# A scheduling priority for the input projection's matmuls in a four-mixer decoder layer

## The chip, the cores and the metric

One core of a Trainium2 chip runs the whole kernel. The metric is device time in microseconds (us); before the change the median of three runs is 2140.05 us (2138.56 to 2140.4). The core has five engines that run side by side, each through its own queue in order: TensorE (PE, matmuls, with its weight loads shown apart as PEld), VectorE (DVE), ScalarE (ACT), GpSimd (POOL) and SyncE (SP, which issues most of the transfers). An engine whose next instruction waits for another engine holds everything behind it in its queue.

## The reference

For 2048 rows of 1024 numbers the reference computes one decoder layer:

```
u     = rmsnorm(x) ;  proj = u @ w_in              # 1024 x 7712
y     = concat( GLA(..), mLSTM(..), HGRN2(..), Mamba-2 SSD(..) )   # 512 columns each
h     = x + y @ w_out ;  out = rmsnorm(h)
```

Each of the four mixers is a causal recurrence over time, computed in chunks: inside a chunk of 128 rows a masked product of queries and keys (scores) times the values, between chunks a state that is decayed and added to. GLA and HGRN2 have a decay for each channel, which the kernel handles by a ladder of levels (1, 2, 4, ... 64 rows apart), each with a small matmul and elementwise rescaling of keys and queries before the next.

## The kernel before

The 2048 rows are worked through in two halves of 1024 rows (8 chunks). In each half ten units run in this order: g0, g1 (GLA, two heads each), s0, s1 (SSD, four heads each), h0 to h3 (HGRN2, one head each), m0, m1 (mLSTM, two heads each). After both halves, the output phase multiplies y by w_out.

A unit has two parts, and in the text of the program the second follows the first.

- **Projections.** Groups of 256 columns of `proj`. Each number is split into a high and a low part, so each product takes three matmuls over 8 slices of the contraction: 24 matmuls for one accumulation. `proj_chan` (line 256) and `proj_chan2` (line 267) put 128 channels by 512 rows in one PSUM bank (tile `ps_c`), four banks and 96 matmuls for a group; `proj_tok` (line 279) puts 128 rows by 256 channels in half a bank (tile `ps_t`, in g0 `ps_g`), 192 matmuls for a group. The PSUM tiles carry the tag `proj`, which has four banks. ACT and DVE move each finished bank into SBUF: an h unit projects `hqf` into `qp`, `kb` and `f`, then `hvz` into `v` and `sz`; an s unit `sx`, `sbc` (through a four-tap convolution, `conv_silu2`) and `sz`; a g unit `gqk`, `gv`, `gz`; an m unit, for each of its two heads, `mqk` and `mvo`, and `mz` at the end. The weights of a group are loaded one group ahead, into two buffers.
- **Products.** What the mixer does with them: `lin_unit` (line 441) for g and h, with tiles `ps_s`, `ps_kt`, `ps_u`, `ps_o`; the loop over 8 chunks in `ssd` (`ps_xt`, `ps_s`, `ps_o`, `ps_u`); the rest of `mlstm`. They use the other four PSUM banks, tag `t`. They are small matmuls, between which DVE and ACT work: each level of `lin_unit` must wait until DVE has rescaled `kb` and `qf`, and that waits until the level before has read them.

SBUF tiles with few buffers tie the units together: `qp`, `kb`, `f` and `v` have two buffers each, `sz` four, `qf` and `pl` one. A g unit takes both `v` buffers; an s unit keeps a `qp`, `kb`, `v` and `f` buffer until its last chunk; an h unit gives `f` back after level 1, `qp` after level 2, `kb` near its end and `v` at its end.

**The order of the work** is not written by hand. Tile's planner makes each engine's queue at build time: it plays the program through with estimated durations, and gives an engine that is free the ready instruction with the lowest priority number. That number is a counter which goes up by one with each instruction of the program's text. So before the change the products of a unit come in front of the next unit's projections whenever they are ready, and a projection runs when no product is.

Of the kernel before, what the change touches and what calls it, by code (L numbers as in the profile page):

```python
# [21 lines left out]
P = 128  # L22
S = 2048
D = 1024
KT = D // P
# [91 lines left out]
class Kernel:  # L117
    def __init__(self, tc, a):
        self.tc, self.nc, self.a = tc, tc.nc, a

    def mm(self, out, l, r, start=True, stop=True, shared=False):

        self.nc.tensor.matmul(out, l, r, start=start, stop=stop, skip_group_check=shared)  # L123
# [132 lines left out]
    def proj_chan(self, w, c, b):  # L256

        hi, lo = w
        ps = self.psp.tile([P, 512], F32, tag="proj", name="ps_c")
        cs = slice(c * P, (c + 1) * P)  # L260
        for k in range(KT):
            self.mm(ps, hi[:, k, cs], self.uh[b][:, k], start=k == 0, stop=False)
            self.mm(ps, hi[:, k, cs], self.ul[b][:, k], start=False, stop=False)
            self.mm(ps, lo[:, k, cs], self.uh[b][:, k], start=False, stop=k == KT - 1)
        return ps

    def proj_chan2(self, w, b):

        hi, lo = w
        pss = [self.psp.tile([P, 512], F32, tag="proj", name="ps_c") for _ in range(2)]  # L270
        for k in range(KT):
            for c, ps in enumerate(pss):
                cs = slice(c * P, (c + 1) * P)
                self.mm(ps, hi[:, k, cs], self.uh[b][:, k], start=k == 0, stop=False)
                self.mm(ps, hi[:, k, cs], self.ul[b][:, k], start=False, stop=False)
                self.mm(ps, lo[:, k, cs], self.uh[b][:, k], start=False, stop=k == KT - 1)
        return pss

    def proj_tok(self, w, ps, t):

        hi, lo = w
        b, ts = t // 4, slice(t % 4 * P, t % 4 * P + P)
        for k in range(KT):
            self.mm(ps, self.uh[b][:, k, ts], hi[:, k], start=k == 0, stop=False)
            self.mm(ps, self.uh[b][:, k, ts], lo[:, k], start=False, stop=False)
            self.mm(ps, self.ul[b][:, k, ts], hi[:, k], start=False, stop=k == KT - 1)

    def proj_tok2(self, w):

# [876 lines left out]
```

## Time and profile before

| | before |
|---|---|
| median of 3 runs | 2140.05 us |
| profiled execution, its own time | 2138.02 us |
| its span, first to last instruction | 2136.2 us |
| granted TensorE clock, mean over the span | 0.994 |
| PE busy | 2095.6 us (98%), 14014 matmuls |
| DVE busy | 1206.0 us (56%) |
| ACT busy | 750.8 us (35%) |

Busy time is the time in which an engine has an instruction of the program in work. Matmuls overlap in the records, so that the sum of their durations is above the busy time; the pace of a run of matmuls is read from a stretch that holds only them. A row of a window gives its start and end, its length, the busy time of PE, PEld, DVE, ACT and POOL with the number of instructions (an engine without any may be missing), the granted clock as a share of full speed, the share of the DMA engines' time, and GB/s; asked for one tile, only the instructions that write or read it are counted.

### The profile page before, as it was taken

Reading aid. Unit: us, or ns where it says so; the run is one execution under the profiler, and the core shown is the slowest. Engines: PE = TensorE matmul, PEld = TensorE weight load, DVE = VectorE, ACT = ScalarE, POOL = GpSimd, SP = SyncE. Lnnn points to the kernel's source line nnn. Section 1 sums busy time; section 2 is a strip of 40 time slices with the busy share of each in tenths; the row PEclk is TensorE's granted clock in tenths of the full one; section 3 lists DMA queues with packets and bytes.
Section 4 is the critical chain, followed back from the end, with each engine's and each line's share of the span. In section 5 each row is a group of like instructions: output and inputs, shape, how many; then the busy total and the mean of one; then the engine's idle time right before and its main releaser. Section 6 shows DMA issues by size and latency. Waiting matters only on the chain.

```text
span 2136.2 us, 35274 instructions
## 1 busy us (share of the span) xinstructions
PE 2095.6 (98%) x14014; PEld 1869.4 (88%) x14014; DVE 1206.0 (56%) x2860; ACT 750.8 (35%) x1885; POOL 62.1 (3%) x96
## 2 busy tenths in 40 slices
PE   8999999999999999999999999999999999999998
PEld 7888889898899999997979889999899998888887
DVE  4564868657676555525366966565654555433332
ACT  6531433444444335442222333333433344212111
POOL 0000011100000000000000211000000000000000
PEclk9999999999999999999999999999999999999999
DMA  8533344444244354442314334322323336423321
GB/s 288 197 94 126 89 152 145 148 140 130 71 130 149 129 159 167 131 143 62 89 51 136 87 105 110 91 82 60 109 90 98 101 109 199 140 80 96 102 74 50
DMA packets 223094, 251.47 MB, mean 118 GB/s; under 512 B 145224, under 2 KB 156600, under 8 KB 211664
## 3 DMA queue, kind: packets, MB, share of 16 engines
q1 hardware_dynamic: 216448, 229.80, 35.3%
q10 hardware_dynamic: 6480, 19.40, 2.6%
q8 instruction: 110, 1.80, 0.3%
q14 instruction: 56, 0.46, 0.1%
HBM read 160.70 MB, written 88.45 MB: 117 GB/s over the span
## 4 chain that ended last, share of the span: by engine, by line
PE 88%; DVE 5%; ACT 3%; DMA 3%; issue 1%; SPq 0%; POOL 0%; ACTq 0%; DVEq 0%; POOLq 0%
PE ps_t L123 30%; PE ps_c L123 25%; PE ps_out L123 15%; PE ps_o L123 6%; PE ps_s L123 5%; PE ps_u L123 3%; PE ps_g L123 2%; DMA ST<-w_out 1%; DMA t2k<-xT 1%; DVE kb L512 1%; DMA hi<-wk 1%; DVE ST L494 0%; ACT t2k L620 0%; DVE ST L557 0%; PE ps_xt L894 0%
## 5 line engine op out<-in xcount | busy, mean ns | idle before, releaser
L123 PE MATMUL ps_t<-hi,uh 128*128 128x256 f32 x1920 | 545.5, 284 | 0.0
L123 PE MATMUL ps_t<-hi,ul 128*128 128x256 f32 x1920 | 544.8, 284 | 0.0
L123 PE MATMUL ps_t<-lo,uh 128*128 128x256 f32 x1920 | 544.3, 284 | 0.0
L123 PEld LDWEIGHTS ps_t<-hi,uh 128*128 128x128 f32 x1920 | 368.0, 192 | 1.6 <-issue 0.7
L123 PEld LDWEIGHTS ps_t<-lo,uh 128*128 128x128 f32 x1920 | 368.1, 192 | 0.9
L123 PEld LDWEIGHTS ps_t<-hi,ul 128*128 128x128 f32 x1920 | 368.0, 192 | 0.3
L123 PE MATMUL ps_c<-uh,hi 128*128 128x512 f32 x896 | 358.7, 400 | 7.4 <-ACT uh L155 7.4
L123 PE MATMUL ps_c<-ul,hi 128*128 128x512 f32 x896 | 357.7, 399 | 0.0
L123 PE MATMUL ps_c<-uh,lo 128*128 128x512 f32 x896 | 356.9, 398 | 0.0
L123 PEld LDWEIGHTS ps_c<-uh,hi 128*128 128x128 f32 x896 | 170.4, 190 | 41.1 <-ACT uh L155 7.8
L123 PEld LDWEIGHTS ps_c<-ul,hi 128*128 128x128 f32 x896 | 170.6, 190 | 34.8 <-DVE ul L156 1.2
L123 PEld LDWEIGHTS ps_c<-uh,lo 128*128 128x128 f32 x896 | 170.5, 190 | 33.9
L305 ACT ACTIVATE v<-ps_t,ss 128x128 f32<-128x128 f32 x128 | 40.4, 363 | 157.8 <-PE ps_t L123 157.7
L976 DVE TENSOR_TENSOR o_sz<-o_sz,ps_out 128x512 f32<-128x512 f32 (+1 forms) x33 | 22.1, 671 | 129.8 <-PE ps_out L123 127.5
L123 PE MATMUL ps_out<-woh,o_qp 128*128 128x512 f32 x288 | 94.3, 396 | 0.5 <-ACT woh L936 0.5
L300 ACT ACTIVATE sz<-ps_t,ss 128x128 f32<-128x128 f32 (+1 forms) x160 | 54.5, 388 | 89.6 <-PE ps_t L123 82.2
L254 DVE TENSOR_TENSOR lo<-raw,hi 128x1024 fp32r<-128x1024 f32 (+1 forms) x58 | 70.5, 1225 | 17.9 <-ACT hi L252 17.0
L301 DVE SCALAR_TENSOR_TENSOR sz<-sz,ps_t 128x256 f32<-128x256 f32 (+1 forms) x80 | 37.5, 471 | 70.6 <-ACT sz L300 70.2
L123 PE MATMUL ps_out<-woh,o_v 128*128 128x512 f32 (+1 forms) x213 | 75.4, 389 | 0.0
L252 ACT CAST hi<-raw 128x512 fp32r<-128x512 f32 (+1 forms) x116 | 65.6, 624 | 25.2 <-PE ps_c L123 19.5
L780 DVE TENSOR_TENSOR t2k<-t2k,ps_s 128x512 f32<-128x512 f32 x16 | 11.0, 688 | 101.3 <-PE ps_s L123 97.2
L123 PEld LDWEIGHTS ps_out<-woh,o_qp 128*128 128x128 f32 x288 | 54.1, 188 | 13.7 <-ACT woh L936 0.9
(357 smaller groups left out, 3549.8 us busy)
## 6 DMA issues: line engine op xcount, KB each, us to landing
raw<-w SPq DMA_DIRECT2D x29, 1024.0 KB, 7.0
wk<-hi SPq DMA_DIRECT2D x29, 1024.0 KB, 4.2
wk<-lo SPq DMA_DIRECT2D x29, 1024.0 KB, 9.5
lo<-wk SPq DMA_DIRECT2D x116, 256.0 KB, 5.5
hi<-wk SPq DMA_DIRECT2D x116, 256.0 KB, 4.7
y<-t2k SPq DMA_DIRECT2D x256, 64.0 KB, 2.0
t2k<-y SPq DMA_DIRECT2D x64, 256.0 KB, 3.4
t2k<-xT SPq DMA_DIRECT2D x32, 256.0 KB, 4.4
```

Source lines behind the costliest of these rows:

```text
L123: self.nc.tensor.matmul(out, l, r, start=start, stop=stop, skip_group_check=shared)
L252: nc.scalar.copy(hi[:, k0:k1], raw[:, k0:k1])
L254: nc.vector.tensor_tensor(lo[:, k0:k1], raw[:, k0:k1], hi[:, k0:k1].bitcast(F32), op=ALU.subtract)
L300: nc.scalar.activation(out[:, j], ps[:, j], AF.Tanh, scale=self.rsh[:, t + j:t + j + 1])
L301: nc.vector.scalar_tensor_tensor(out=out, in0=out, scalar=1.0, in1=ps, op0=ALU.add, op1=ALU.mult)
L305: self.nc.scalar.activation(out[:, j], ps[:, j], AF.Identity, scale=sc[:, t + j:t + j + 1])
L512: nc.vector.tensor_tensor(kv[:, :, 0], kv[:, :, 0], pv[:, :, 1:2].to_broadcast([P, n, b]), op=ALU.mult)
L780: nc.vector.tensor_tensor(dt, dt, ps, op=ALU.mult)
L976: nc.vector.tensor_tensor(xt[:, ns], xt[:, ns], ps, op=ALU.add)
```

## The change

The three functions that issue projection matmuls open a guard around them. Inside the guard the planner's counter is set back by 500; when the guard is left it stands again where it stood on entry. Nothing is computed otherwise, no instruction is added or removed, and the copies out of PSUM, the weight loads and the products keep their own numbers.

```diff
+    def ahead(self):
+
+        return self.tc.high_priority(offset=500)
...
     def proj_chan(self, w, c, b):
...
-        for k in range(KT):
-            self.mm(ps, hi[:, k, cs], self.uh[b][:, k], start=k == 0, stop=False)
-            self.mm(ps, hi[:, k, cs], self.ul[b][:, k], start=False, stop=False)
-            self.mm(ps, lo[:, k, cs], self.uh[b][:, k], start=False, stop=k == KT - 1)
+        with self.ahead():
+            for k in range(KT):
+                self.mm(ps, hi[:, k, cs], self.uh[b][:, k], start=k == 0, stop=False)
+                self.mm(ps, hi[:, k, cs], self.ul[b][:, k], start=False, stop=False)
+                self.mm(ps, lo[:, k, cs], self.uh[b][:, k], start=False, stop=k == KT - 1)
         return ps
```

`proj_chan2` and `proj_tok` get the same guard around their loops.

## Rows read from the trace of the kernel before

**Rows 1.** The page: busy time by engine, the span in 40 slices, the chain's shares

```profile
PE 2095.6 (98%) x14014; PEld 1869.4 (88%) x14014; DVE 1206.0 (56%) x2860; ACT 750.8 (35%) x1885; POOL 62.1 (3%) x96
...
PE   8999999999999999999999999999999999999998
...
PE 88%; DVE 5%; ACT 3%; DMA 3%; issue 1%; SPq 0%; POOL 0%; ACTq 0%; DVEq 0%; POOLq 0%
```

**Rows 2.** Waits of PE, longest first: total us, times, longest

```profile
PE ps_s L123 <- DVE kb L512: 9.6, 7, 2.2
PE ps_c L123 <- ACT uh L155: 7.4, 2, 6.0
PE ps_s L123 <- DVE craw L734: 2.7, 1, 2.7
```

**Rows 3.** Timeline of PE in h1's products: start, duration us, count

```profile
525.79 0.94 PE L123 MATMUL ps_s<-qf,t2k 128*128 128x128 f32 x7
...
528.49 1.13 PE L123 MATMUL ps_s<-qf,t2k 128*128 128x128 f32 x8
...
531.16 1.13 PE L123 MATMUL ps_s<-qf,t2k 128*128 128x128 f32 x8
```

**Rows 4.** Timeline of DVE, the first instruction of two units' products

```profile
498.57 1.27 DVE L450 TENSOR_TENSOR qf<-qp,f 128x1024 f32<-128x1024 f32 x1 [0.27 <-PE ps_o L123]
...
546.45 1.27 DVE L450 TENSOR_TENSOR qf<-qp,f 128x1024 f32<-128x1024 f32 x1
```

**Rows 5.** Windows of g0's, s0's, h1's products: length, busy by engine, clock, DMA

```profile
98.00:143.70 45.70, 42.80 (x460) 36.22 (x458) 28.31 (x58) 11.65 (x37) 0.00 (x0) 0.96 0.39 136
...
281.90:342.00 60.10, 60.04 (x317) 50.70 (x316) 53.70 (x119) 21.99 (x48) 10.74 (x14) 1.00 0.44 139
...
522.40:546.40 24.00, 23.50 (x192) 22.22 (x191) 16.13 (x35) 10.90 (x36) 0.00 (x0) 1.00 0.35 112
```

**Rows 6.** Of `ps_c` alone, in products of g0, g1, s0, s1, h3, m0's first head

```profile
98.00:143.70 45.70, 18.39 (x65) 12.79 (x65) 0.00 (x0) 3.12 (x4) 0.96 0.39 136
186.40:234.70 48.30, 23.49 (x87) 16.43 (x87) 2.05 (x3) 0.00 (x0) 0.96 0.19 67
281.90:342.00 60.10, 43.14 (x180) 33.38 (x181) 4.08 (x6) 0.00 (x0) 1.00 0.44 139
367.90:433.00 65.10, 22.97 (x97) 17.92 (x98) 1.37 (x2) 2.37 (x2) 1.00 0.37 124
...
619.40:645.10 25.70, 15.44 (x53) 9.44 (x54) 1.38 (x2) 0.00 (x0) 1.00 0.38 123
676.10:689.20 13.10, 5.87 (x20) 3.54 (x21) 0.00 (x0) 0.00 (x0) 1.00 0.67 220
```

**Rows 7.** Of `ps_t` alone, in products of g0, s1, h1, m0's second head

```profile
98.00:143.70 45.70, 4.14 (x30) 3.77 (x30) 0.00 (x0) 0.00 (x0) 0.96 0.39 136
...
367.90:433.00 65.10, 24.51 (x194) 23.48 (x192) 1.92 (x4) 4.49 (x14) 1.00 0.37 124
522.40:546.40 24.00, 11.56 (x79) 10.00 (x80) 0.82 (x2) 2.49 (x8) 1.00 0.35 112
...
729.60:742.80 13.20, 5.92 (x40) 4.90 (x39) 0.00 (x0) 1.14 (x4) 1.00 0.69 228
```

**Rows 8.** A stretch with `ps_c` alone on PE

```profile
761.50:783.00 21.50, 21.50 (x96) 17.70 (x95) 2.04 (x3) 0.00 (x0) 1.00 0.64 196
```

**Rows 9.** A stretch with `ps_t` alone on PE

```profile
783.30:806.10 22.80, 22.80 (x192) 22.80 (x191) 0.00 (x0) 3.43 (x12) 1.00 0.60 209
```

**Rows 10.** From g0's decays to its first level: all engines

```profile
60.00:100.00 40.00, 37.84 (x298) 34.98 (x296) 23.51 (x51) 29.24 (x45) 0.95 (x1) 1.00 0.45 169
```

**Rows 11.** Three stretches of 3 us in g0's levels: all engines, granted clock

```profile
106.00:109.00 3.00, 1.79 (x8) 1.13 (x6) 3.00 (x10) 1.50 (x5) 0.00 (x0) 1.00 1.01 421
109.00:112.00 3.00, 2.35 (x34) 2.21 (x35) 1.48 (x3) 0.38 (x1) 0.00 (x0) 0.98 0.14 57
112.00:115.00 3.00, 3.00 (x9) 2.32 (x8) 2.15 (x4) 0.00 (x0) 0.00 (x0) 0.50 0.00 0
```

More of the change, by code (lines that the diff above doesn't have):

```diff
@@ L270, in proj_chan2 @@
         pss = [self.psp.tile([P, 512], F32, tag="proj", name="ps_c") for _ in range(2)]
[L271 to L276, printed above, removed]
+        with self.ahead():
+            for k in range(KT):
+                for c, ps in enumerate(pss):
+                    cs = slice(c * P, (c + 1) * P)
+                    self.mm(ps, hi[:, k, cs], self.uh[b][:, k], start=k == 0, stop=False)
+                    self.mm(ps, hi[:, k, cs], self.ul[b][:, k], start=False, stop=False)
+                    self.mm(ps, lo[:, k, cs], self.uh[b][:, k], start=False, stop=k == KT - 1)
         return pss
@@ L282, in proj_tok @@
         b, ts = t // 4, slice(t % 4 * P, t % 4 * P + P)
[L283 to L286, printed above, removed]
+        with self.ahead():
+            for k in range(KT):
+                self.mm(ps, self.uh[b][:, k, ts], hi[:, k], start=k == 0, stop=False)
+                self.mm(ps, self.uh[b][:, k, ts], lo[:, k], start=False, stop=False)
+                self.mm(ps, self.ul[b][:, k, ts], hi[:, k], start=False, stop=k == KT - 1)
     def proj_tok2(self, w):
```

## The prediction

> **What bounds the kernel now.** I read the page first: PE is busy 2095.6 of 2136.2 us, no slice of the span falls under eight tenths, and 88% of the chain that ended last is PE [rows 1]. So PE sets the end, and 40.6 us is all that a better order can win. PE's list of waits comes second. Its two largest entries are 9.6 us on the level ladder's `kb` and 7.4 us on the splitting of the first rows of x [rows 2]; the third is 2.7 us, so in its steady part PE waits for nothing, and a projection is always ready. Third, the timeline inside the products of one h unit. The level matmuls come as groups of eight that take 1.13 us, and their starts lie 2.7 us apart [rows 3]: between two groups DVE and ACT rescale `kb` and `qf`, and in that time PE runs `ps_t`. The products are thus a serial chain that leaves PE free for more than half of its time, and projections fill the holes. The first DVE instruction of h1's products starts the moment h0's last `ps_o` ends, and that of the next unit 47.9 us later [rows 4]: with one `qf`, the chains of two units do not overlap. Fourth, busy time in the stretches of such chains. Over s0's 60.1 us PE is busy 60.04 and DVE 53.70, over h1's 24.0 us PE is busy 23.50 and DVE 16.13 [rows 5]. How much of that is filling is seen when the projection tiles are asked for alone [rows 6, 7].
>
> **What the change moves.** Matmuls, their durations, the copies, the transfers and the bytes all stay. What moves is PE's order. The counter does not go up for what is inside the guard, so 500 spans 500 other instructions. Counted in the program's text, a unit has without its projection matmuls: g0 507, g1 364, s 345, h 230, an m head 170. The last 313 of g0 and g1, 246 of s, 178 of h and 95 of a head are its products. For an h unit i that gives: the projections of i+1 stand some 260 to 230 numbers in front of its start, and those of i+2 at 460+9-500 = -31 to 460+46-500 = +6, where its products begin at 52. Both units ahead outrank the whole chain. In the same way g0's products and gates lie behind all of g1; s1's behind h0 and h1; the first half of s0's chain is in front of h0 and the second behind; an m head is behind the next two.
>
> The planner therefore lets projections run until a buffer stops them, and only then the chain. What stops them is known: the unit two ahead finds `qp`, `kb`, `f` or `v` taken, so its matmuls go as far as the four `proj` banks, and stop. Four banks are one group: 21.5 us of `ps_c`, at 21.50/96 = 0.224 us each [rows 8], or 22.8 us of `ps_t`, at 22.80/192 = 0.119 us [rows 9]. These used to be the filling; now they are spent in front of the chain, where DVE and ACT have little to do, and the holes stay open. The cost is the filling that each chain has now and loses, less what buffers still allow inside it:
>
> - g0: 65 `ps_c` and 30 `ps_t`: 65 x 0.224 + 30 x 0.119 = 18.1 us. `gqk` of g1 and four banks of its `gv` go ahead, and g0 holds both `v` buffers: nothing is left to fill with. 18.1.
> - g1: 87 x 0.224 = 19.5 us. `sx` of s1 ranks behind the first half of this chain and can fill 21.5 us. 0.
> - s0: 180 x 0.224 = 40.3 us. Only `hqf` of h0 can fill, into banks: 40.3 - 21.5 = 18.8.
> - s1: 97 x 0.224 + 194 x 0.119 = 44.8 us. Both h0 and `hqf` of h1 are in front: 44.8.
> - h: 53 x 0.224 = 11.9 us in h3, 79 x 0.119 = 9.4 in h1; the mean 10.65 for four units is 42.6. After level 2 `qp` comes free, `hqf` of i+2 leaves its banks and `hvz` takes them, again in front of the rest of the chain, and then waits for `v`.
> - m: 20 x 0.224 = 4.5 us and 40 x 0.119 = 4.8 us; 4.65 for four heads is 18.6. With `mqk` and `mvo` two heads ahead parked, they are lost.
>
> All counts are from [rows 6, 7]. One half loses 18.1 + 18.8 + 44.8 + 42.6 + 18.6 = 142.9 us; the second half runs the same ten units, so 285.8 us. The profiled execution took 2138.0 us, so 2138.0 + 285.8 = 2423.8; it lies 2.0 us under the median of the runs shown, hence 2425 us. Of the present idle 40.6 us I count nothing as won.
>
> Four costs the rows don't show as such. (a) g0's decays and gates need matmuls between 60 and 100 us, where PE is busy 37.84 of 40 us, mostly with `gz` and `gqk` as filling [rows 10]; with these first, a half loses between 0 and the 33 us that they take. (b) After g1 the convolutions of s0 finish on DVE with the banks full: 0 to the 18.8 us already lost in s0. (c) The first two levels of an h unit lie outside the stretches counted: 0 to 2 x 2.7 us each [rows 3]. (d) ACT, DVE and SP keep their numbers, and copies out of PSUM find idler engines than today; nothing is queued behind a new wait on them, but PE's own queue is in order, so a projection that waits for a late bank on the chip holds the chain behind it: bounded by the hole between two level groups, 2.7 - 1.13 = 1.6 us [rows 3], 0 to 1.6 us for each of some 60 groups, 96 us. I take 0 for all, since in each case DVE has work to do meanwhile; at a third of their tops (a) to (c) add 2 x (11 + 6 + 7) = 48 us, and the range keeps that and half of (d). Below, a chain that finds DVE and ACT free may be shorter: DVE is busy 53.70 of s0's 60.1 us [rows 5] also with weight splits and convolutions that now fall elsewhere.
>
> The clock speaks against the change too. In g0's levels PE has 1.79 busy us in 3, and 3 us later its granted clock is 0.50, the lower of its two levels, 1.2 GHz, for a stretch of nine matmuls [rows 11], after which it is back. Chains without filling have such holes all along. The Trainium skill, page "TensorE: Matmul & The Clock Gate", section "HAM oscillation — how this bites in real kernels", tells of a kernel whose waits between bursts of matmuls throw the clock back to half each time; the trace agrees in that one place. By that rule every open hole of a chain would be followed by slow matmuls, and the sum would be that of the last rival below.
>
> **Rivals.** *Only the next unit gets in front, or the banks of the unit after it still fill.* If a parked group were spent inside the chain, h and m would lose nothing, s1 44.8 - 21.5 = 23.3, s0 18.8 and g0 18.1 us: 60.2 a half, 120 in all, 2260 us. For it: a blocked projection costs no time, and the DVE parts of a chain could run while the group is in front. Against it: the count of -31 to +6 above.
>
> *Faster.* The chain's DVE and ACT steps catch up while projections run, so its matmuls then stand ready in a row, and PE idles less than today. It decides if after the change less than 40.6 us of PE's span is idle. The price: the ladder's 9.6 us and about as much again at half clock [rows 2, 11] go, 2140 - 20 = 2120 us. For it: an m head has only 4.5 us of filling in 13.1 [rows 6], near to that. Against: a level can't be readied before the one in front of it is read, and starts 2.7 us apart [rows 3] show it.
>
> *No change*: some buffer (weights, `sz`) already holds projections back as much as the new rank could push them. 2140 us. Against: no such wait stands at the head of PE's list [rows 2].
>
> *Worse, by the clock.* The chains' own matmuls fill 45.70 - 18.1 - 2.9 (idle) = 24.7 us in g0, 60.1 - 40.3 = 19.8 in s0 and 24.0 - 9.4 - 0.5 = 14.1 in h1 [rows 5 to 7]. With g0, s0, s1 and four h units that is some 121 us a half; if all of it took half as long again, 2 x 60 = 121 us come on top, 2546 us.
>
> **How the numbers follow.** Forecast (2330 to 2500 us): 0.50. Milder, around 2260 (2160 to 2330): 0.22. Worse, around 2546: 0.12. Faster, around 2120: 0.12. No change: 0.04. What a measurement of this kernel can tell from no change is about 0.2%. All of the first three are slower: 0.84; same 0.04; faster 0.12. The range runs from 2165, the foot of the milder case, to 2560: the worse case plus what of (a) to (d) does not overlap with it. The likeliest case alone has 2330 to 2500.
>
> **What would show it.** Right: PE's share falls from 98% to between 84 and 90%, its busy time stays near 2096 us, and PE's waits list `ps_s` and `ps_o` on DVE and ACT with some 280 us in sum, the most in s1's and s0's chunks. The timeline of an h unit shows `ps_t` and `ps_c` in one piece and then groups of eight `ps_s` with nothing between. The granted clock's mean falls under 0.98. Wrong: projections still between the levels; idle PE under `ps_c` or `ps_t` waiting for weights (then the step on what stops them fails); or idle under 40 us. The sum is off if the holes of h or m are filled and those of s are not, which the second rival would show.

## The result, and the profile after

The changed kernel takes 2651.74 us (median of four runs, 2651.36 to 2655.5), the kernel before in the runs beside it 2140.23 us: 1.239 times as long, [1.238, 1.241]. It is slower, as forecast, but by 512 us where 285 were forecast, and the time lies 92 us above the top of the range. The profiled execution took 2651.36 us; its span is 2649.6 us, and the mean granted clock 0.911 (before 0.994).

The page of the changed kernel: busy time by engine, PE and the granted clock in 40 slices, the chain's shares. They answer to [rows 1].

```profile
PE 2278.4 (86%) x14014; PEld 2002.4 (76%) x14014; DVE 1188.7 (45%) x2860; ACT 728.1 (27%) x1877; POOL 58.8 (2%) x96
...
PE   8869998878888788887799888798787889799998
...
PEclk9869999879988898998699999798888999799999
...
PE 74%; DVE 14%; ACT 6%; DMA 3%; issue 2%; SPq 0%; POOL 0%; ACTq 0%; DVEq 0%; POOLq 0%
```

Two terms are to be read here. PE idles 2649.6 - 2278.4 = 371.2 us, where it idled 40.6: 330.6 us more. And PE is busy 2278.4 us where it was busy 2095.6, for the same 14014 matmuls: 182.8 us more. Their sum is the whole growth of the span, 513.4 us. The second term was not in the sum of the forecast. In the chain that ended last DVE and ACT have risen from 8% to 20%.

PE's waits after: engine, tile and what it waits for, then total us, times, longest. They answer to [rows 2].

```profile
PE ps_s L127 <- DVE qf L520: 65.8, 38, 2.8
PE ps_o L127 <- DVE t2k L914: 57.9, 20, 5.3
PE ps_u L127 <- DVE t2k L797: 41.7, 12, 11.3
PE ps_u L127 <- ACT t2k L593: 19.6, 20, 2.0
PE ps_s L127 <- DVE kb L519: 14.8, 5, 3.7
PE ps_c L127 <- DVE rs_t L142: 13.2, 2, 6.6
...
PE ps_t L127 <- DVE f L711: 12.5, 2, 6.3
```

`ps_s` on `qf` is the ladder of g and h, `ps_o` on `t2k` the chunks of s, `ps_u` on line 797 the heads of m. The last two are of another kind: projections that wait.

The timeline of PE in h1 of the changed kernel (start, duration, then idle time before it and what ended it). The first row is a level; behind it stand 96 matmuls of `ps_t`, 712.7 to 724.9 us, not shown.

```profile
710.32 1.06 PE L127 MATMUL ps_s<-qp,t2k 128*128 128x128 f32 x8
...
724.72 1.05 PE L127 MATMUL ps_s<-qf,t2k 128*128 128x128 f32 x8
727.31 1.13 PE L127 MATMUL ps_s<-qf,t2k 128*128 128x128 f32 x8 [1.54 <-DVE qf L520]
729.98 1.13 PE L127 MATMUL ps_s<-qf,t2k 128*128 128x128 f32 x8 [1.54 <-DVE qf L520]
732.64 2.04 PE L127 MATMUL ps_s<-qf,t2k 128*128 128x128 f32 x8 [1.54 <-DVE qf L520]
735.56 2.04 PE L127 MATMUL ps_s<-qf,t2k 128*128 128x128 f32 x8 [0.88 <-DVE qf L520]
...
739.19 2.08 PE L127 MATMUL ps_u<-v,t2k 128*128 128x128 f32 x8 [0.73 <-ACT t2k L593]
```

This is the picture that was foretold: the filling in one piece, then groups of eight with nothing between. The starts still lie 2.7 us apart, as in [rows 3], so an idle PE makes the chain no faster. And it shows the term that was missed: after three holes of 1.54 us the same eight matmuls take 2.04 us instead of 1.13, at a granted clock of 0.50 (from 731.4 to 745.1 us). The same is seen in s1's chunks, where each chunk waits for DVE:

```profile
519.37 1.64 PE L127 MATMUL ps_o<-t2k 128*128 128x64 f32 x8 [2.71 <-DVE t2k L914]
...
523.23 0.39 PE L127 MATMUL ps_s<-ct,v 128*128 128x128 f32 x2
527.80 1.97 PE L127 MATMUL ps_o<-t2k 128*128 128x64 f32 x8 [4.20 <-DVE t2k L914]
...
532.02 0.63 PE L127 MATMUL ps_s<-ct,v 128*128 128x128 f32 x2
535.94 1.97 PE L127 MATMUL ps_o<-t2k 128*128 128x64 f32 x8 [3.29 <-DVE t2k L914]
```

Windows of the changed kernel, with the columns of [rows 5]: g0's levels, chunks of s1, products of h0 and of h1. The column behind POOL is the granted clock.

```profile
154.00:198.00 44.00, 26.19 (x285) 24.00 (x284) 22.13 (x36) 6.32 (x14) 0.00 (x0) 0.61 0.21 72
...
520.00:566.00 46.00, 27.64 (x99) 23.30 (x98) 24.25 (x67) 7.42 (x20) 8.64 (x12) 0.61 0.31 98
...
642.60:665.20 22.60, 15.03 (x98) 13.11 (x96) 12.20 (x27) 10.06 (x30) 0.00 (x0) 0.85 0.41 141
707.70:749.80 42.10, 33.39 (x220) 30.60 (x218) 19.90 (x39) 16.19 (x43) 0.00 (x0) 0.84 0.27 93
```

In [rows 5] the products of g0, s0 and h1 ran at 0.96, 1.00 and 1.00 with PE busy nearly throughout. Now the clock is 0.61 where PE is busy 27.64 of 46 us. A mean of 0.911 between the levels 2.4 and 1.2 GHz says that (1 - 0.911) / 0.5 = 18% of the span ran at the lower one, where it was 1.2%.

Not all of the 182.8 us can be the clock. Counted in the trace, 311.1 us of PE's busy time lie in stretches at the lower clock, where it was 20.4. At most half of such time is lost to the clock, so its part is at most (311.1 - 20.4) / 2 = 145 us; if all of it slowed like the eight matmuls above, from 1.13 to 2.04 us, some 130 us (an estimate). What the other 40 to 50 us are stays open. Overlap that neighbouring matmuls lose at a hole is a candidate: PE's work falls into 198 pieces with idle time between them, where it was 56.

Groups of PE after (line, operation, shapes, count; busy us, mean ns of one; idle us before them and what ended it):

```profile
L127 PE MATMUL ps_t<-hi,uh 128*128 128x256 f32 x1920 | 507.3, 290 | 43.8 <-DVE f L711 12.5
...
L127 PE MATMUL ps_c<-uh,hi 128*128 128x512 f32 x896 | 340.8, 411 | 52.9 <-DVE rs_t L142 13.2
...
L127 PE MATMUL ps_s<-qf,t2k 128*128 128x128 f32 x320 | 64.9, 367 | 53.6 <-DVE qf L520 47.1
...
L127 PE MATMUL ps_o<-t2k 128*128 128x64 f32 x256 | 45.8, 334 | 57.9 <-DVE t2k L914 57.9
```

The same groups in the kernel before:

```profile
L123 PE MATMUL ps_t<-hi,uh 128*128 128x256 f32 x1920 | 545.5, 284 | 0.0
...
L123 PE MATMUL ps_c<-uh,hi 128*128 128x512 f32 x896 | 358.7, 400 | 7.4 <-ACT uh L155 7.4
...
L123 PE MATMUL ps_s<-qf,t2k 128*128 128x128 f32 x320 | 44.6, 282 | 1.0
...
L123 PE MATMUL ps_o<-t2k 128*128 128x64 f32 x256 | 33.7, 274 | 2.0 <-DVE t2k L907 1.8
```

A level matmul takes 367 ns on the mean (282 before), a projection 290 and 411 (284 and 400): the lower clock falls mostly on the chains, since the projections now come in long unbroken runs. If the busy time is split by tile over all PE instructions, about 129 of the 183 us are in product tiles (133.5 to 179.7 in `ps_s`, 130.0 to 180.4 in `ps_o`, 56.9 to 79.3 in `ps_u`), about 48 in projections. Split the same way, PE idles 82.8 us more in front of `ps_s`, 72.6 in front of `ps_u`, 60.1 in front of `ps_o`, and 91.6 more in front of projections.

A wait of another kind stands at m0's first head. PE's last `ps_kt` ends at 941.7 us; the timeline then has these rows among those of all engines:

```profile
943.74 0.68 DVE L614 TENSOR_TENSOR sz<-sz,ps_o 128x512 f32<-128x512 f32 x1
...
950.44 0.71 DVE L645 STREAM_TRANSPOSE t2k<-sz 128x512 f32<-128x512 f32 x1
951.08 1.09 DVE L781 SCALAR_TENSOR_TENSOR t2k<-mb,g_a,cf 128x128 f32<-128x128 f32 x4
952.09 0.68 DVE L797 TENSOR_TENSOR t2k<-ps_kt,g_kw 128x512 f32<-128x512 f32 x1
...
952.92 2.06 PE L127 MATMUL ps_u<-v,t2k 128*128 128x129 f32 x8 [11.26 <-DVE t2k L797]
```

From 943.7 to 951.1 us DVE finishes the unit before (norm, scaling, transposes), which has the lower numbers; only then come the head's decays. Before the change projections ran in that time, and PE did not idle in this head; now it has none left to run.

### The profile page after: what moved, and what is told of

It is laid out like the page before. It is cut to its first block, busy times and chain, and to the rows that moved or that the text cites. A ratio compares the mean times of both kernels' runs of the same rounds, so it can differ in the third digit from the quotient of the medians.

```text
span 2649.6 us, 35277 instructions
## 1 busy us (share of the span) xinstructions
PE 2278.4 (86%) x14014; PEld 2002.4 (76%) x14014; DVE 1188.7 (45%) x2860; ACT 728.1 (27%) x1877; POOL 58.8 (2%) x96
## 4 chain that ended last, share of the span: by engine, by line
PE 74%; DVE 14%; ACT 6%; DMA 3%; issue 2%; SPq 0%; POOL 0%; ACTq 0%; DVEq 0%; POOLq 0%
PE ps_t L127 25%; PE ps_c L127 21%; PE ps_out L127 13%; PE ps_o L127 5%; PE ps_s L127 5%; PE ps_u L127 2%; PE ps_g L127 2%; DVE qf L520 1%; ACT t2k L627 1%; DMA ab<-rows 1%; DMA t2k<-xT 1%; DVE t2k L912 1%; DVE lo L258 1%; DVE kb L519 1%; DMA lo<-wk 1%
## 5 line engine op out<-in xcount | busy, mean ns | idle before, releaser
L127 PE MATMUL ps_t<-hi,uh 128*128 128x256 f32 x1920 | 507.3, 290 | 43.8 <-DVE f L711 12.5
L127 PE MATMUL ps_t<-lo,uh 128*128 128x256 f32 x1920 | 498.2, 286 | 0.4 <-DMA lo<-wk 0.4
L127 PE MATMUL ps_t<-hi,ul 128*128 128x256 f32 x1920 | 494.6, 285 | 0.0
L127 PE MATMUL ps_c<-ul,hi 128*128 128x512 f32 x896 | 328.4, 404 | 1.9 <-DVE ul L160 1.9
L127 PE MATMUL ps_s<-qf,t2k 128*128 128x128 f32 x320 | 64.9, 367 | 53.6 <-DVE qf L520 47.1
L127 PE MATMUL ps_u<-v,t2k 128*128 128x128 f32 (+1 forms) x256 | 44.4, 327 | 68.4 <-DVE t2k L797 41.7
L127 PEld LDWEIGHTS ps_s<-qf,t2k 128*128 128x128 f32 x320 | 56.5, 266 | 60.6 <-issue 43.6
L745 DVE TENSOR_TENSOR craw<-ps_c,rb 128x512 f32<-128x512 f32 x64 | 43.4, 686 | 124.5 <-PE ps_c L127 124.4
L127 PEld LDWEIGHTS ps_u<-v,t2k 128*128 128x128 f32 x256 | 37.7, 226 | 76.7 <-issue 35.1
L127 PE MATMUL ps_o<-t2k 128*128 128x64 f32 x256 | 45.8, 334 | 57.9 <-DVE t2k L914 57.9
```

What stands on the lines that cost most here:

```text
L745: nc.vector.tensor_tensor(rw, ps, self.rb[:, b * 512:(b + 1) * 512], op=ALU.mult)
```

## The experiments

Theory A is the prediction's, with the clock added: PE's rank alone does it, holes stay open where projections outrank a chain, and each open hole brings half-clock matmuls with it. Against it stands in each experiment the rival that its expectation names; the one that returns is the prediction's (d), that a projection which waits in PE's queue for a late bank holds the chain behind it. All eleven kernels, ratios against runs of the kernel before beside them; PE's idle time is span less busy, from the page of each:

| kernel | median us | ratio, 95% | PE idle | PE busy | clock |
|---|---|---|---|---|---|
| before | 2140 | | 40.6 | 2095.6 | 0.994 |
| after (500) | 2651.74 | 1.239 [1.238, 1.241] | 371.2 | 2278.4 | 0.911 |
| off250 | 2282.47 | 1.067 [1.061, 1.072] | 104.4 | 2179.4 | 0.975 |
| off100 | 2198.03 | 1.026 [1.023, 1.029] | 73.1 | 2124.1 | 0.984 |
| off30 | 2146.06 | 1.0044 [1.0029, 1.0059] | 43.7 | 2097.9 | 0.997 |
| honly | 2319.56 | 1.084 [1.080, 1.088] | 150.0 | 2167.4 | 0.957 |
| noth | 2491.17 | 1.164 [1.158, 1.170] | 259.9 | 2225.8 | 0.936 |
| notg | 2579.64 | 1.207 [1.205, 1.210] | 325.6 | 2248.7 | 0.925 |
| prodfirst | 2181.31 | 1.019 [1.015, 1.024] | 55.8 | 2124.6 | 0.987 |
| evict | 2609.79 | 1.218 [1.210, 1.225] | 343.9 | 2270.1 | 0.912 |
| copies | 2135.79 | 0.9996 [0.9986, 1.0005] | 37.2 | 2095.8 | 0.994 |
| warm | 2607.59 | 1.217 [1.211, 1.222] | 249.0 | 2353.2 | 0.953 |
| before_warm | 2271.01 | 1.060 [1.056, 1.063] | 39.8 | 2229.9 | 0.998 |

**How far up: off250, off100, off30.** Only the number in the guard changes, to 250, 100 and 30.

```diff
-        return self.tc.high_priority(offset=500)
+        return self.tc.high_priority(offset=250)
```

> The guard sets the counter back by 250 in place of 500, so that a projection of an h unit's next unit still stands in front of the whole chain of products (230+9-250 = -11), but that of the unit after it no longer does (460+9-250 = 219 of 230). Theory A (rank: the chains lose the projections of two units as filling): per half g0 loses about 12 us, s0 19, s1 23, h 0, m 9, so 126 us of open holes in all, and with 0.55 us of slower matmuls for each us of hole, as in the changed kernel (183 to 331 us), some 2335 us (2290 to 2380), granted clock 0.96. Theory B (queue: PE's order rests on estimates that are off, and blocks on late copies whenever projections are far in front): nearly all of the 511 us remain, over 2500 us.

> The guard sets the counter back by 100. A projection then stands in front of no more than the last 40% of the chain ahead of it (h: 230+9-100 = 139 of 52 to 230; s: 254 of 91 to 345; g: 416 of 194 to 507), and the unit after the next never. Theory A: each chain keeps enough filling, 2135 to 2165 us, clock 0.98 or more. Theory B (blocking in PE's queue): a fifth of the 511 us, 2240 us.

> The guard sets the counter back by 30 instead of 500, so that only the last 30 numbers of a unit's products are outranked. Theory A (the cost is about linear in the part of a chain that is outranked; 100 cost 56 us, 250 cost 140 us): 17 us, 2150 to 2165 us. Rival B (at 100 the cost is that of a few places, the start of a half above all, which 30 does not reach): 2135 to 2148 us, no wait of ps_c on DVE's o_sz.

At 250, a little over the length of an h unit, 369 us of the 512 are gone. The idle time of PE in the h units is 4.3 us over both halves, where it was 114. That is A's point on the count: only when both units ahead outrank a chain is there nothing left to fill it with. B is refuted, but the time also lies 8 us under A's range, and not by A's terms: PE idles 63.8 us more than before, where A put 126, and its busy time grew by 83.8 us, where A put 69. In stretches at the lower clock PE is busy 84.4 us, 64 more than before, so that at most 32 of these 83.8 us are the clock; the rest stays open. At 100 the time lies between the two numbers, so A alone doesn't hold there. PE's waits of off100:

```profile
PE ps_c L127 <- DVE o_sz L308: 20.0, 2, 10.0
PE ps_s L127 <- DVE kb L519: 12.4, 5, 3.8
```

Twice, at the start of each half, a projection of g1 stands 10.0 us in PE's queue waiting for a bank that ACT and DVE have not emptied; it is the largest wait of off100. That could be the queue's mechanism, but no held work is to be seen. The first product behind it, `ps_r` of line 385, gets its input from DVE at about 102 us, and the wait ended at 97.3 us; in the second half it is 1005.8 after 1001.1. ACT, which delivers to DVE, was at work nearly throughout. So the filling had run out, and B's mechanism isn't shown here. At 30 that wait is absent and the time within 9 us of before: B's number for off30, not the 17 us of a cost that is linear in the offset. It is still slower than before, by 0.44%.

**Which units: honly, noth, notg.** The guard sets back by 500 in some units only; the loop over units notes the kind.

```diff
-        return self.tc.high_priority(offset=500)
+        return self.tc.high_priority(offset=500 if self.unit == "h" else 0)
...
+                            self.unit = u[0]
```

noth has `!= "h"` in that place, notg `!= "g"`.

> Only the projections of the h units are set back by 500; those of g, s and m pass the guard with 0, so that the counter still leaves them out. Theory A: the h chains lose their filling (42.6 us a half) and s1 loses its own (44.8 us a half) to h0 and h1; s0 is filled by s1 again, g and m as before. 175 us of holes, with 0.55 us of slow matmuls for each 270 us: 2410 us (2360 to 2450). Theory B: the cost goes with the number of projections in front, 288 of the 480, 384, 288 and 405 matmuls a unit, about 0.37 of 511 us: 2330 us.

> The other part alone: the projections of g, s and m are set back by 500, those of h by 0. Theory A: g0 loses 18, s0 some 19 of its 40 (h0's group is behind it and fills), s1 none (h0 fills it), h3 its filling and m its own, about 18 + 19 + 11 + 19 = 67 us a half, 134 us of holes, 207 us with the slow matmuls: 2350 us (2280 to 2400). The two parts, this one and that with h alone, would add up to 480 us of the 511 if each chain pays for its own filling. Theory B: 0.63 of 511 us, 2460 us.

> The guard sets back by 500 in s, h and m units and by 0 in g units. Theory A (costs of the kinds of units add up; g's units hold 66 us of the 321 us that PE's idle time grew by, and with the half-clock matmuls each idle us costs 1.55 us): 102 us less than the changed kernel, 2520 to 2580 us. Rival B (a unit's own holes are opened by the projections of the units behind it, so that g1's stay open by s0's rank and only g0's close): 2590 us or more.

honly costs 181 us and noth 352, together 533; all units at once cost 512. So the costs add up, within 4%. But both times lie outside A's ranges and nearer to B's numbers: A gave too much to h and too little to the rest. B's share for h is miscounted: an m unit has 768 projection matmuls, not 405, so h has 1152 of the 4416 of a half, 0.26, and B gives some 2272 and 2517 us. The times lie between the two theories and decide for neither. The sizes of A's terms are refuted here, its places are not. The holes of honly are where A puts them: 62 us idle in h units and 44 in s1, in whose two stretches 812 and 819 projection matmuls now run (492 and 454 before), over 600 of them in front of its second chunk and 192 in front of its last, while g and m stand nearly as before. noth has its largest waits in m, s and g (`ps_u` on line 797, 44.2 us; `ps_o` on line 914, 40.5; `ps_s` on `qf`, 30.1). notg comes out 72 us below the changed kernel, on the upper edge of A's range, and its trace shows why it isn't more: g0's chain closes (18.1 us of idle become 3.3), but g1, which stood at 4.0 and 3.3 us before and at 5.3 and 5.4 in the changed kernel, idles 4.8 and 16.1. That a unit's holes are opened by the projections of the units behind it is seen in g0, which g1's projections no longer outrank; for g1, which s0's still do, it is argued, since only its second half idles more.

**Rank on PE or rank on the copies: prodfirst, evict, copies.** prodfirst leaves the projections at 500 and sets the products' matmuls and transposes back by 1500, so that they win on PE again. evict keeps the change and sets the copies out of PSUM back by 500 as well. copies sets these back alone, with the projections as before the change.

```diff
+    def pm(self, out, l, r, start=True, stop=True, shared=False):
+        with self.tc.high_priority(offset=1500):
+            self.nc.tensor.matmul(out, l, r, start=start, stop=stop, skip_group_check=shared)
...
-                    self.mm(ps[:, c], kb[r, c * C:(c + 1) * C], q[r, c])
+                    self.pm(ps[:, c], kb[r, c * C:(c + 1) * C], q[r, c])
```

> The change stays, and the matmuls and transposes of the products, which come after the projections in a unit, are set back by 1500, so that they stand in front of every projection again; copies, elementwise work and transfers keep their numbers. Theory A (PE's rank between products and projections is all that matters): the time of the kernel before, 2130 to 2160 us, clock 0.99. Rival: what costs is that the counter now leaves out the projections, which shifts DVE, ACT, SP and the buffers too: over 2250 us.

```diff
-            self.nc.scalar.activation(out[:, j], ps[:, j], AF.Identity, scale=sc[:, t + j:t + j + 1])
+        with self.ahead():
+            self.nc.scalar.activation(out[:, j], ps[:, j], AF.Identity, scale=sc[:, t + j:t + j + 1])
```

> The changed kernel, in which the copies of projection banks out of PSUM (on ACT and DVE) get the same 500. PE is idle for some 100 us right in front of projection matmuls in the changed kernel, against 7.5 in the kernel before. Theory A (a parked group waits for a buffer of the unit two in front of it, and its copies are short): little changes, 2620 to 2670 us. Rival (the copies stand behind other work on ACT and DVE because their numbers stayed): at least 50 us of that idle time goes, under 2600 us.

> The matmuls keep the order of the kernel before; only the copies of projection banks out of PSUM (on ACT and DVE) are set back by 500. Theory A (PE bounds the kernel before, with 40 us of idle PE at most, and PE's rank alone is what costs): 2125 to 2150 us, PE's idle time 20 to 50 us. Rival B (DVE and ACT ranks matter as much as PE's, since a copy that comes in front of a level's rescaling holds the chain): slower by over 1%, from 2162 us on, with waits of ps_s on DVE's qf and kb in PE's list.

prodfirst gets 470 of the 512 us back, though the projections keep their 500. Its 2181 us are 21 above A's range and under the rival's 2250. PE in h1 of prodfirst, between whose levels projections run again:

```profile
523.72 1.16 PE L137 MATMUL ps_s<-qf,t2k 128*128 128x128 f32 x8
...
526.63 1.13 PE L137 MATMUL ps_s<-qf,t2k 128*128 128x128 f32 x8
...
529.45 1.05 PE L137 MATMUL ps_s<-qf,t2k 128*128 128x128 f32 x8
```

No row has idle time in front of it, and no group takes 2.04 us. So it is the order of products and projections on PE that costs 470 us. Of the other 42 us 15 are idle time and 29 busy time; what they are is open, and the rival's shift of the other engines may be in them. evict falls between the two numbers: PE's idle time in front of `ps_c` and `ps_t` goes from 99.1 to 67.8 us, so about a third of that part came from banks that DVE and ACT emptied late. The rest of the idle time stays. copies makes no difference: here, where PE bounds, the rank of the copies is worth nothing.

**The clock: warm, before_warm.** 320 useless matmuls of 128x256 (two in front of each h level, one per head in front of each g level, six in front of each s chunk's `ps_o`) write to a bank that the products overwrite. In the trace they are 640 instructions, since a product of f32 numbers stands there as two. warm has them on top of the change, before_warm on the kernel before.

```diff
+    def warm(self, ps, n):
+        for _ in range(n):
+            self.mm(ps, self.cf[:, :P], self.cf[:, :2 * P])
...
+                    self.warm(po[:, :2 * P], 6)
```

> The changed kernel with useless matmuls in the holes of the chains: of 128x256 f32 on constants, written to the bank that the products overwrite next, two ahead of each level in h, one a head in g, six ahead of each s chunk's ps_o. At 0.6 us for such a matmul (the ps_u of an s chunk) that is 58 + 19 + 115 = 192 us of work that the changed kernel doesn't have. Theory A (the 183 us by which PE's busy time grew are matmuls at the lower clock, which follows from the holes): the granted clock rises from 0.91 to 0.94 or more and the time falls, to 2540 to 2620 us, in spite of the added work. Rival (the growth is the latency of matmuls that stand alone, whatever the clock): the time stays or rises, 2640 to 2840 us.

> The same useless matmuls in the kernel before, where projections fill the holes. Theory A: PE has no room for them, the time rises by most of their 192 us, 2290 to 2340 us, clock 0.99. If it rose by under 60 us, PE would not be what bounds the kernel before.

On the kernel before these matmuls cost 2229.9 - 2095.6 = 134.3 us of PE's busy time and 129 us of the median. That is under the range expected, since a filler is cheaper than was put, but nearly all of its busy time reaches the end: PE was the bound, as [rows 1] were read. On the changed kernel the same work takes the time down by 44 us. The page of warm:

```profile
PE 2353.2 (90%) x14654; PEld 2055.8 (79%) x14654; DVE 1189.8 (46%) x2860; ACT 729.2 (28%) x1877; POOL 58.6 (2%) x96
...
PEclk9879999999999988999899999999999999899999
```

The granted clock rises from 0.911 to 0.953. Less the fillers' 134.3 us PE's own work is busy 2218.9 us, 59.5 less than in the changed kernel; idle time and fillers together are 12 us more. So the gain is in the work itself. Its groups show the same (columns as above):

```profile
L127 PE MATMUL ps_s<-qf,t2k 128*128 128x128 f32 x320 | 49.9, 305 | 20.9 <-DVE qf L528 19.5 <-ACT t2k L475 1.4
...
L127 PE MATMUL ps_o<-t2k 128*128 128x64 f32 x256 | 34.6, 271 | 3.9 <-DVE t2k L922 3.9
```

A level matmul takes 305 ns (367 without fillers, 282 before), one of s's `ps_o` 271 (334, 274). Sorted by the granted clock at its start, a level matmul takes 283 ns at full clock in the changed kernel, as before the change, and 437 at the lower one; 175 of the 320 start at the lower clock, 48 in warm and none before. So the longer matmuls are the clock's, and the rival, latency whatever the clock, is refuted for them. warm is not a clean measure of the clock's size, since the filler instructions count in the planner's numbers and shift the order somewhat. None of the eleven kernels beats the kernel before.

## Why the prediction missed its range

- **PE bounds the kernel before**: right. before_warm pays nearly the whole of what is added.
- **The count: both units ahead outrank a chain**: right. At 250 the holes of h are closed, at 500 open, and h1's timeline has the form foretold. The rival in which a parked group still fills (2260 us) is refuted for 500; that off250 comes close to it (2282) is luck, since over half of what off250 costs is busy time.
- **The idle time, 286 us from the filling lost**: measured 330.6, of which some 320 in the units. By kind of unit, both halves, forecast and measured: g 36 and 66, s 127 and 81, h 85 and 112, m 37 and 60. The sum is 15% off and the parts more; that they offset each other is luck. s is too high, and the sign that s would idle most failed with it: buffers come free during its first chunks, and 384 to 480 projection matmuls still run within the stretch of each s unit (454 to 492 before). The others are too low because of what was set to zero: g's chains lose 33 us against 36, and another 33 lie in front of g0's chain, where (a) had put them; in h four waits of 6.6 us, each of a projection right behind a unit's last product, make up nearly all of the 27 us that were missing.
- **(a) to (d) at zero**: wrong, though within their tops in sum: 45 us more idle time than was counted. (d) bounded each wait of a projection by the 1.6 us of a hole; single waits came to 6.6 and 10.0 us in the changed kernel, and PE idles 91.6 us more in front of `ps_c` and `ps_t`. That ready work stood behind such a wait is not shown. A part not listed is a unit's end on DVE, as in m0's first head (11.3 us).
- **The clock left out of the sum**: this step failed. The sign "busy time stays near 2096 us" is refuted by 2278.4; the growth of 182.8 us, of which some 130 and at most 145 are the clock, is more than the 92 us to the top of the range. The row that told of it had been read: nine matmuls at 0.50 after a stretch of holes [rows 11]. Another sign, a mean clock under 0.98, came true and contradicted the sum: over 2425 us it is 97 us at the lower clock. The term was put into a rival with 0.12 and priced at 121 us, from the chains of g0, s0, s1 and h, with g1, m and the projections left out and half as much time again for a slow matmul, where 2.04 for 1.13 us is 1.8 times. That was near the clock's part; the rival fell short of the run by the idle time above and by the busy time that is open. 2138.0 + 286 + 45 + 183 gives the 2652 us of the run: the first mechanism a little under its size, the second missing.

The two terms go together. Over the kernels with more than 200 us of added idle time, the busy time grew by 0.54 to 0.59 of it (after 182.8 on 330.6, noth 130.2 on 219.3, notg 153.1 on 285.0, evict 174.5 on 303.3); honly has 71.8 on 109.4. With little idle time the ratio doesn't hold: off250 has 83.8 on 63.8, off100 28.5 on 32.5, prodfirst 29.0 on 15.2, which stays open. The Trainium skill, page "TensorE: Matmul & The Clock Gate", section "HAM oscillation — how this bites in real kernels", tells of a kernel that waits some 3 to 5 us for a transfer after each burst of matmuls and starts the next burst at half clock. The trace goes the same way with holes that DVE sets: eight matmuls at 1.13 us and, after three holes of 1.54 us, at 2.04. That holes as short as these suffice is shown by this trace and not stated there, so the prediction's "every open hole" went beyond the page.

That the four buffers `qp`, `kb`, `f` and `v` are what stops the projections two units ahead rests on the count and on the timelines. It is not shown: a third buffer of each, which would test it, wasn't tried.

## What to carry to other kernels

On an engine that bounds the kernel, work that can run at any time should rank behind a serial chain that can't: put in front, it is not done sooner in sum, and the chain's holes have nothing left to fill them. When holes are to open on TensorE, count them and then the matmuls between them at half clock as well; here PE's busy time grew by 0.55 us for each idle us, most of it by the clock. A priority offset is to be compared with the length of a unit in the planner's own numbers: at 30 it cost 0.4%, at 100 2.6%, at 250 6.7%, at 500 24%.

## What the runs showed of the hardware

- Holes of 1.54 us between groups of eight matmuls of 1.13 us sufficed for the lower clock in h1 of the changed kernel; in [rows 3], with `ps_t` in those holes, the same groups kept 1.13 us.
- A level matmul took 283 ns at full clock and 437 at the lower one in the changed kernel; at full clock it took 282 before the change.
- Added matmuls can make a kernel faster: 320 of them, worth 129 us where PE is full, took 44 us off where it was not.
